# A hybrid encoder layer in three-product fp32: one of the weight sums of the seven-product pairs moved from VectorE to an accumulating GpSimd transfer, and the split of the sums it belongs to moved to the end

## The chip, the cores and the metric

One core of one Trainium2 chip runs the whole layer in one launch. The metric is the device time of that launch in microseconds (us), lower is better. Beside the plain times there is one profiled execution, from which all rows below are taken.

The core's engines are named as in the profile: PE is TensorE's matmuls (PEld its weight loads), DVE is VectorE, ACT is ScalarE, POOL is GpSimd, SP is the engine whose queue issues the loads. Each engine works through its own instructions in a fixed order and waits on semaphores for the others.

## The reference

The input is `x` of 256 tokens by 2048 float32. The layer is: a SwiGLU feed-forward block, a mixer (a gated linear recurrence beside a windowed attention, between one input and one output projection), and a second SwiGLU block, each between two RMS norms:

```python
def swiglu(x, w_gate_up, w_down):
    gate, up = jnp.split(x @ w_gate_up, 2, axis=-1)
    return (jax.nn.silu(gate) * up) @ w_down
...
ff = swiglu(rms_norm(x, pre_norm_ffn1[layer]), w_ffn1_gate_up[layer], w_ffn1_down[layer])
x = x + 0.5 * rms_norm(ff, post_norm_ffn1[layer])
h = rms_norm(x, pre_norm_mix[layer])
... # recurrence and attention on h @ w_mix_in[layer]
mixed = jnp.concatenate([y_h.astype(x.dtype), y_a.astype(x.dtype)], axis=-1) @ w_mix_out[layer]
x = x + rms_norm(mixed, post_norm_mix[layer])
# and the second SwiGLU block, again with 0.5
```

The weights are what is large: `w_ffn*_gate_up` is 2048 x 11264 and `w_ffn*_down` 5632 x 2048, twice, `w_mix_in` 2048 x 6656, `w_mix_out` 2048 x 2048, all float32.

## The kernel before

**Three products for one.** The matmuls run in fp32r (a float32 rounded to fewer bits). Each operand is therefore split into a high part `h`, rounded by ACT, and a low part `l`, the rest, which DVE takes (`split_act`, lines 176 and 177). A product of two operands is then three matmuls, h by h, h by l and l by h (`Blocks.three`, line 441). All weights have to be loaded from HBM, rounded by ACT and subtracted by DVE before PE can use them.

**Units.** The two feed-forward projections and the output projection work in units of 256 rows of the weight (two tiles of 128 rows) by 1024 columns (two blocks of 512). One unit is one `raw` tile of 128 partitions by 2048 columns that holds the four blocks b11, b12, b21, b22 side by side. There are three buffers for `raw`, five for `h` and five for `l` tiles of 1024 columns (a half of a `raw` tile each). `load` is issued on SP's queue when a `raw` buffer comes free.

A plain unit (`Blocks.plain`) multiplies eight times: two tokens' halves m, two column blocks n, two row tiles k. With three matmuls each that is 24 matmuls, and two split halves.

**Seven-product pairs.** Some units (the mixed ones: units 2, 4 and 6 of the eight of a gate/up group, ten of 22 in each run of the down projection, two of eight in each run of the output projection) are done with Winograd's form of Strassen's scheme, in `Blocks.seven`: seven products instead of eight, 21 matmuls, for sums of the left and of the right operand. The left sums are kept. The sums of the weights have to be made for each pair, in place in `raw`:

- b11 is split first, alone (`one_block`). 
- Line 473 is one DVE instruction on 1024 columns: b11 becomes b11 + b12, and b12 becomes b12 + b22.
- `lower` is the split of the second half of `raw`, still b21 and b22.
- Line 477 makes b22 = b11 + b22, with the new b11.
- `upper` is the split of the first half, b11 + b12 and b12 + b22.
- Line 479 makes b21 = b22 + b21, with the new b22.
- `last` is the split of the second half again, now with the sums.

So the four `h`/`l` tiles of a pair are those of b11, `lower`, `upper` and `last`, in this order, and PE multiplies in this order too: p0 with b11, two products with `lower`, two with `upper`, two with `last`.

**The order of the work.** Outside of a few hand-written stretches a scheduler decides at build time in which order each engine's instructions stand; on the chip the order is fixed. `aside` is a call that puts the load and the first split of the next unit between the steps of a pair; it is used where the next unit is a plain one and belongs to the same call of `work`, which is so in the down and output projections and not in the gate/up groups, whose units are called one by one.

**A gate/up group** is one pass of the eight units over 1024 columns (512 of gate, 512 of up). There are eleven groups in each feed-forward block. At the group's end `fold` adds the seven products to the banks of the plain ones: ACT copies one bank (line 522) and DVE does eight additions (lines 516 to 539), of which line 520 is the last that reads the product banks. Then the gate goes through Silu and times up (lines 959 and 960), PE transposes the result, and it is split for the down projection, with its sums (lines 395 to 399).

**GpSimd** does little: a few small loads and constants at the start and mid-layer, and the powers for the norms.

Of the kernel before, what the change touches and what calls it, by code (L numbers as in the profile page):

```python
# [17 lines left out]
ALU = mybir.AluOpType  # L18
AX = mybir.AxisListType

P = 128
# [16 lines left out]
def hymba_layer_kernel(  # L38
# [25 lines left out]
    nc = tc.nc  # L64
# [11 lines left out]
    def nm(s):  # L76
        uid[0] += 1
        return f"{s}_{uid[0]}"

    def pa():  # L80
        return psum.tile([P, 512], F32, tag="pa", name=nm("pa"))

    def pb():
        return psum.tile([P, 512], F32, tag="pb", name=nm("pb"))
# [56 lines left out]
    def load(src, between=None):  # L141
        raw = rawp.tile([P, 2048], F32, tag="raw", name=nm("raw"))
        if len(src.shape) == 4:

            dst = raw.rearrange("p (a n b) -> p a n b", a=src.shape[1], n=src.shape[2])
            parts = [(dst[:, a], src[:, a]) for a in range(src.shape[1])]
        else:
            parts = [(raw.rearrange("p (a b) -> p a b", a=src.shape[1]), src)]
        for i, (to, of) in enumerate(parts):
            if i and between:  # L150
                between()
            nc.sync.dma_start(to, of)
        return raw
# [14 lines left out]
    def split_half(raw, i, hp=hip, lp=lop):  # L168
        part = raw[:, i * 1024 : (i + 1) * 1024]
        h = hp.tile([P, 1024], F32R, tag="h", name=nm("h"))  # L170
        l = lp.tile([P, 1024], F32R, tag="l", name=nm("l"))
        split_act(h, l, part)
        return h, l

    def split_act(hi, lo, src):
        nc.scalar.copy(hi, src)  # L176
        nc.vector.tensor_tensor(lo, src, hi.bitcast(F32), ALU.subtract)  # L177
# [37 lines left out]
    last = {}  # L215
# [175 lines left out]
    S2, S3, S4, S1 = range(4)  # L391
# [10 lines left out]
    class Blocks:  # L402
# [60 lines left out]
        def seven(self, u, aside=None):  # L463

            raw = load(self.source(u))
            if aside:
                aside()
            b11, b12, b21, b22 = (raw[:, i * 512 : (i + 1) * 512] for i in range(4))
            four = raw.rearrange("p (i c) -> p i c", i=4)
            h, l = self.one_block()  # L470
            split_act(h, l, b11)

            nc.vector.tensor_tensor(  # L473
                four[:, 0:2], four[:, 0::3], four[:, 1:2].to_broadcast([P, 2, 512]), ALU.add
            )
            lower = split_half(raw, 1)
            nc.vector.tensor_tensor(b22, b11, b22, ALU.add)
            upper = split_half(raw, 0)
            nc.vector.tensor_tensor(b21, b22, b21, ALU.add)  # L479
            if aside:  # L480
                aside()
            last = split_half(raw, 1)
            if not self.p:
                self.p = [pa(), pa(), pb(), pb()]
            a, w = self.tiles[u], self.left_sums(u)

            def lhs(k, m):
                return [a[:, k, i, m * P : (m + 1) * P] for i in range(2)]

            def summed(j):  # L490
                return [w[:, j, i, :] for i in range(2)]

            def rhs(two, n):
                return [x[:, n * 512 : (n + 1) * 512] for x in two]

            for at, left, right in (
                (("p", 0), lhs(0, 0), (h, l)),
                (("c", 0, 0), lhs(1, 0), rhs(lower, 0)),
                (("c", 0, 1), summed(S4), rhs(lower, 1)),
                (("p", 1), summed(S1), rhs(upper, 0)),  # L500
                (("p", 3), summed(S3), rhs(upper, 1)),
                (("p", 2), summed(S2), rhs(last, 1)),
                (("c", 1, 0), lhs(1, 1), rhs(last, 0)),
            ):
                self.three(at, *left, *right)

# [79 lines left out]
    class Pairs(Blocks):  # L586
# [24 lines left out]
        def source(self, u):  # L611
            src = self.w[u * 2 * P : (u + 1) * 2 * P, self.now * 1024 : (self.now + 1) * 1024]
            return src.rearrange("(k p) c -> p k c", p=P)

        def left_sums(self, u):
            if u in self.kept:
                return self.kept[u]
            keep = self.now == 0 and u in self.keep
            if keep and u in self.near:
                w = self.room.tile([P, 4, 2, P], F32R, tag="sp", name=nm("sp"), bufs=3)  # L620
            else:
                tag = f"sp{u}" if keep else "sp"
                w = far["pool"].tile([P, 4, 2, P], F32R, tag=tag, name=nm("sp"), bufs=1 if keep else 2)
            split_act(w[:, :, 0, :], w[:, :, 1, :], self.sums[u])
            if keep:
                self.kept[u] = w
            return w
# [222 lines left out]
    class Gated(Blocks):  # L850
# [10 lines left out]

        def source(self, u):
            return self.w[:, 2 * u : 2 * u + 2, :, self.g * 512 : (self.g + 1) * 512]

        def left_sums(self, u):
            return self.sums[u]
# [171 lines left out]
    with tc.manual_schedule():  # L1038
# [9 lines left out]
        raw = rawp.tile([P, 2048], F32, tag="raw", name=nm("raw"))  # L1048
# [121 lines left out]
    with ExitStack() as s2:  # L1170
# [399 lines left out]
        rows = Pairs(w_mix_out[0], orders, yt, ysums, yroom, post_norm_mix)  # L1570
# [84 lines left out]
```

## Time and profile before

| what | value |
|---|---|
| median of 3 runs | 1836.45 us (1835.72 to 1837.55) |
| the profiled execution: span from first to last instruction | 1835.7 us |
| the profiled execution's own time beside that span | not listed apart from it; the span lies 0.75 us below the median |
| mean granted TensorE clock in it | 0.999 |
| PE busy | 1821.5 us (99%) |
| DVE busy | 1620.7 us (88%) |
| ACT busy | 1099.7 us (60%) |
| POOL busy | 23.3 us (1%) |
| DMA engines, loads of SP's queue | 56.0% of 16 engines' span, 364.17 MB |
| instructions of line 473, one for each seven-product pair | 102 |

The busy time of an engine is the time in which at least one of its instructions runs. Matmuls overlap in PE's pipeline, so that "99% busy" only says that there was hardly a moment without one. In the rows of groups the columns are line, engine, operation, tiles out<-in with their shapes, and count; then busy us and mean ns of one; then idle time before them and what ended it. In a timeline a row is a start in us, a duration in us, engine, line, operation, tiles, and xN where N instructions follow each other without a gap; in brackets stands the engine's idle time before it and its releaser.

### The profile page before, as it was taken

Reading aid. Unit: us, or ns where it says so; the run is one execution under the profiler, and the core shown is the slowest. Engines: PE = TensorE matmul, PEld = TensorE weight load, DVE = VectorE, ACT = ScalarE, POOL = GpSimd, SP = SyncE. Lnnn points to the kernel's source line nnn. Section 1 sums busy time; section 2 is a strip of 40 time slices with the busy share of each in tenths; the row PEclk is TensorE's granted clock in tenths of the full one; section 3 lists DMA queues with packets and bytes.
Section 4 is the critical chain, followed back from the end, with each engine's and each line's share of the span. In section 5 each row is a group of like instructions: output and inputs, shape, how many; then the busy total and the mean of one; then the engine's idle time right before and its main releaser. Section 6 shows DMA issues by size and latency. Waiting matters only on the chain.

```text
span 1835.7 us, 22980 instructions
## 1 busy us (share of the span) xinstructions
PE 1821.5 (99%) x8492; PEld 1516.5 (83%) x8492; DVE 1620.7 (88%) x2047; ACT 1099.7 (60%) x1454; POOL 23.3 (1%) x39
## 2 busy tenths in 40 slices
PE   9999999999999999999999999999999999999998
PEld 7888888888888888888888888888888888888786
DVE  7989999999999998477787798989999999999897
ACT  7555555555666567476587556455556555566563
POOL 1000000000000001000000000000000000000000
PEclk9999999999999999999999999999999999999999
DMA  7555555556555576555454456555555555545564
GB/s 255 206 178 213 207 200 191 184 188 215 205 208 216 195 260 212 199 182 174 163 170 150 167 210 224 190 195 190 213 193 192 213 212 195 205 187 206 201 229 177
DMA packets 174737, 365.77 MB, mean 199 GB/s; under 512 B 9256, under 2 KB 44160, under 8 KB 173856
## 3 DMA queue, kind: packets, MB, share of 16 engines
q1 hardware_dynamic: 174272, 364.17, 56.0%
q8 instruction: 66, 1.08, 0.2%
q14 instruction: 47, 0.39, 0.1%
q0 software_dynamic: 352, 0.14, 0.0%
HBM read 360.06 MB, written 4.21 MB: 198 GB/s over the span
## 4 chain that ended last, share of the span: by engine, by line
PE 94%; ACT 2%; DVE 2%; DMA 1%; issue 0%; POOL 0%; DVEq 0%; SPq 0%; ACTq 0%; POOLq 0%
PE pa L441 40%; PE pb L441 36%; PE pa L309 5%; PE pa L314 3%; PE pa L364 2%; PE pa L362 2%; PE pa L363 2%; DMA raw<-in_w_ffn_down_dram 1%; DVE l L177 1%; ACT h L176 1%; PE pb L971 1%; PE pa L971 1%; PE pb L1376 0%; PE pb L1350 0%; PE pb L1454 0%
## 5 line engine op out<-in xcount | busy, mean ns | idle before, releaser
L176 ACT CAST h<-raw 128x1024 fp32r<-128x1024 f32 (+1 forms) x825 | 821.5, 1021 | 538.2 <-PE pb L441 146.9
L177 DVE TENSOR_TENSOR l<-raw,h 128x1024 fp32r<-128x1024 f32 (+1 forms) x825 | 950.1, 1180 | 135.7 <-ACT h L176 106.0
L441 PE MATMUL pa<-h,xt 128*128 128x512 f32 x1176 | 409.5, 390 | 0.1
L441 PE MATMUL pb<-h,xt 128*128 128x512 f32 x1060 | 376.9, 392 | 0.0
L441 PEld LDWEIGHTS pa<-h,xt 128*128 128x128 f32 x1176 | 220.8, 188 | 46.1 <-DVE xt L232 0.6
L441 PEld LDWEIGHTS pb<-h,xt 128*128 128x128 f32 x1060 | 199.0, 188 | 41.6 <-DVE pb L537 0.6
L441 PE MATMUL pa<-l,xt 128*128 128x512 f32 x588 | 229.2, 390 | 0.0
L441 PE MATMUL pb<-l,xt 128*128 128x512 f32 x530 | 206.4, 389 | 0.0
L441 PE MATMUL pb<-h,ht 128*128 128x512 f32 x464 | 163.5, 390 | 0.0
L441 PE MATMUL pa<-h,ht 128*128 128x512 f32 x464 | 162.7, 389 | 0.0
L441 PEld LDWEIGHTS pa<-l,xt 128*128 128x128 f32 x588 | 110.4, 188 | 23.4 <-DVE l L177 0.8
L473 DVE TENSOR_TENSOR raw<-raw 128x1024 f32<-128x1024 f32 x102 | 124.3, 1219 | 1.1
L309 PE MATMUL pa<-xt,h 128*128 128x512 f32 x512 | 124.4, 393 | 0.2 <-ACT h L176 0.2
L441 PEld LDWEIGHTS pb<-l,xt 128*128 128x128 f32 x530 | 99.6, 188 | 19.6
L309 PEld LDWEIGHTS pa<-xt,h 128*128 128x128 f32 x512 | 93.8, 188 | 18.6 <-ACT h L176 0.6
L441 PEld LDWEIGHTS pa<-h,ht 128*128 128x128 f32 x464 | 87.1, 188 | 18.1
L441 PEld LDWEIGHTS pb<-h,ht 128*128 128x128 f32 x464 | 87.1, 188 | 18.0
L441 PE MATMUL pb<-l,ht 128*128 128x512 f32 x232 | 90.3, 389 | 0.0
L441 PE MATMUL pa<-l,ht 128*128 128x512 f32 x232 | 90.3, 389 | 0.0
L441 PE MATMUL pa<-h,xs 128*128 128x512 f32 x232 | 80.8, 389 | 0.0
L441 PE MATMUL pb<-h,xs 128*128 128x512 f32 x232 | 80.8, 389 | 0.0
L479 DVE TENSOR_TENSOR raw<-raw 128x512 f32<-128x512 f32 x102 | 70.1, 688 | 1.8
(281 smaller groups left out, 2360.6 us busy)
## 6 DMA issues: line engine op xcount, KB each, us to landing
raw<-in_w_ffn_gate_up_dram SPq DMA_DIRECT2D x350, 512.0 KB, 4.7
raw<-in_w_ffn_down_dram SPq DMA_DIRECT2D x88, 1024.0 KB, 5.0
raw<-in_w_mix_in_dram SPq DMA_DIRECT2D x52, 1024.0 KB, 4.9
raw<-in_w_mix_out_dram SPq DMA_DIRECT2D x16, 1024.0 KB, 4.9
pg<-in_post_norm_ffn_dram SPq DMA_DIRECT2D x4, 512.0 KB, 7.4
X<-in_x_dram SPq DMA_DIRECT2D x2, 1024.0 KB, 8.4
bias<-row SPq DMA_DIRECT2D x16, 128.0 KB, 5.0
kept<-X SPq DMA_DIRECT2D x2, 1024.0 KB, 4.1
```

What stands on the lines that cost most here:

```text
L176: nc.scalar.copy(hi, src)
L177: nc.vector.tensor_tensor(lo, src, hi.bitcast(F32), ALU.subtract)
L309: nc.tensor.matmul(slot[f], weights(hs, kk, f), xcol(xt, k), start=(k == 0), stop=(k == KT - 1))
L314: nc.tensor.matmul(slot[f][:, 0:T], weights(ls, kk, f), xcol(xt, kh * 8 + kk, 0), start=False, stop=False,)
L362: nc.tensor.matmul(dst, xh, h[:, o : o + n], start=(k == 0), stop=False)
L363: nc.tensor.matmul(dst, xh, l[:, o : o + n], start=False, stop=False)
L364: nc.tensor.matmul(dst, xl, h[:, o : o + n], start=False, stop=(k == KT - 1))
L441: nc.tensor.matmul(self.bank(at), lhs, rhs, start=(n == 1), stop=n in (ends, self.of[at]), skip_group_check=n > ends,)
L473: nc.vector.tensor_tensor(four[:, 0:2], four[:, 0::3], four[:, 1:2].to_broadcast([P, 2, 512]), ALU.add)
L479: nc.vector.tensor_tensor(b21, b22, b21, ALU.add)
L971: nc.tensor.transpose(bank[:, o : o + P], zs[m][:, k * P : (k + 1) * P], ident)
```

## The change

The one DVE instruction of line 473 becomes one of half its width, b11 = b11 + b12, and an accumulating transfer issued by GpSimd: it reads the block b22 (128 x 512 float32, 256 KB) from HBM a second time and adds it to b12 in SBUF. It depends on the addition before it, which reads b12, and the split `upper` depends on it. The split `upper` is put behind the split `last`, and the second `aside` behind `last` too. The order of the products follows: the two with `last` come ahead of the two with `upper`. A new method `block` gives the address of one 128 x 512 block for each of the two kinds of weight.

```diff
             h, l = self.one_block()
             split_act(h, l, b11)
 
-            nc.vector.tensor_tensor(
-                four[:, 0:2], four[:, 0::3], four[:, 1:2].to_broadcast([P, 2, 512]), ALU.add
-            )
+            nc.vector.tensor_tensor(b11, b11, b12, ALU.add)
+            nc.gpsimd.dma_start(b12, self.block(u, 1, 1), accum_op=ALU.add)
             lower = split_half(raw, 1)
             nc.vector.tensor_tensor(b22, b11, b22, ALU.add)
-            upper = split_half(raw, 0)
             nc.vector.tensor_tensor(b21, b22, b21, ALU.add)
+            last = split_half(raw, 1)
             if aside:
                 aside()
-            last = split_half(raw, 1)
+            upper = split_half(raw, 0)
...
                 (("c", 0, 1), summed(S4), rhs(lower, 1)),
+                (("c", 1, 0), lhs(1, 1), rhs(last, 0)),
+                (("p", 2), summed(S2), rhs(last, 1)),
                 (("p", 1), summed(S1), rhs(upper, 0)),
                 (("p", 3), summed(S3), rhs(upper, 1)),
-                (("p", 2), summed(S2), rhs(last, 1)),
-                (("c", 1, 0), lhs(1, 1), rhs(last, 0)),
...
+        def block(self, u, k, n):
+            rows, cs = (2 * u + k) * P, self.now * 1024 + n * 512
+            return self.w[rows : rows + P, cs : cs + 512]
...
+        def block(self, u, k, n):
+            return self.w[:, 2 * u + k, n, self.g * 512 : (self.g + 1) * 512]
```

In the changed kernel the three additions stand at lines 472, 475 and 476 and the transfer at line 473; the lines of `fold` move up by two, those behind `block` move down by three and five. In the order that the scheduler makes of it, the instructions of PE, DVE and ACT are as many as before, and `upper` stands in each pair where `last` stood, on DVE, on ACT and on PE.

More of the change, by code (lines that the diff above doesn't have):

```diff
@@ L468, in seven @@
             b11, b12, b21, b22 = (raw[:, i * 512 : (i + 1) * 512] for i in range(4))
-            four = raw.rearrange("p (i c) -> p i c", i=4)
             h, l = self.one_block()
             split_act(h, l, b11)
-            nc.vector.tensor_tensor(
-                four[:, 0:2], four[:, 0::3], four[:, 1:2].to_broadcast([P, 2, 512]), ALU.add
-            )
+            nc.vector.tensor_tensor(b11, b11, b12, ALU.add)
+            nc.gpsimd.dma_start(b12, self.block(u, 1, 1), accum_op=ALU.add)
             lower = split_half(raw, 1)
             nc.vector.tensor_tensor(b22, b11, b22, ALU.add)
-            upper = split_half(raw, 0)
             nc.vector.tensor_tensor(b21, b22, b21, ALU.add)
+            last = split_half(raw, 1)
             if aside:
                 aside()
-            last = split_half(raw, 1)
+            upper = split_half(raw, 0)
             if not self.p:
```

## The prediction

> **What bounds the kernel now.** I read the page's busy times and its chain of waits first, then the busy times of whole stages, then the timelines of DVE, ACT and PE over one gate/up group.
>
> ```profile
> PE 1821.5 (99%) x8492; PEld 1516.5 (83%) x8492; DVE 1620.7 (88%) x2047; ACT 1099.7 (60%) x1454; POOL 23.3 (1%) x39
> PE 94%; ACT 2%; DVE 2%; DMA 1%; issue 0%; POOL 0%; DVEq 0%; SPq 0%; ACTq 0%; POOLq 0%
> ```
>
> ```profile
> 50.00:480.00 430.00, 430.00 (x1937) 356.49 (x1936) 397.54 (x462) 243.90 (x280) 0.00 (x0) 1.00 0.56 200
> 480.00:720.00 240.00, 239.34 (x1067) 197.41 (x1067) 229.48 (x276) 147.06 (x192) 1.58 (x3) 1.00 0.59 216
> 1110.00:1590.00 480.00, 479.85 (x2174) 397.75 (x2173) 438.72 (x542) 274.93 (x351) 3.06 (x4) 1.00 0.55 197
> 1590.00:1822.00 232.00, 230.72 (x1021) 190.40 (x1020) 219.03 (x249) 137.62 (x164) 0.00 (x0) 1.00 0.56 209
> 358.79:401.16 42.37, 42.37 (x192) 35.18 (x192) 39.42 (x48) 24.42 (x29) 0.00 (x0) 1.00 0.56 199
> ```
>
> The columns of the windows are length, then busy time and count of PE, PEld, DVE, ACT and POOL, then clock, DMA share and GB/s. The first two rows are the gate/up groups and the down runs of the first feed-forward block, the next two those of the second, the last is one gate/up group. PE is without a gap in the gate/up groups, and lacks 0.66 + 0.15 + 1.28 us in the other three stretches. 94% of the chain is PE. A busy PE could still be a slow one, so I look at its starts.
>
> ```profile
> 357.02 0.39 PE L441 MATMUL pa<-h,xt 128*128 128x512 f32 x1
> 357.25 0.39 PE L441 MATMUL pb<-h,xt 128*128 128x512 f32 x1
> 357.48 0.39 PE L441 MATMUL pa<-h,xt 128*128 128x512 f32 x1
> ```
>
> They follow at 0.23 us. A group has 3 pairs of 21 matmuls and 5 plain units of 24, 183 in all; at 0.2265 us that is 41.4 us of the group's 42.37, and the transposes fill the rest. So the group is as long as its matmuls, and DVE, though 93% busy (39.42 of 42.37), runs just ahead of PE. What relieves DVE is worth nothing here beyond the 2.1 us that PE lacks, 0.1% of the time; what delays DVE by more than its lead is paid in full.
>
> **The change, part by part.** The DVE work:
>
> ```profile
> L473 DVE TENSOR_TENSOR raw<-raw 128x1024 f32<-128x1024 f32 x102 | 124.3, 1219 | 1.1
> L479 DVE TENSOR_TENSOR raw<-raw 128x512 f32<-128x512 f32 x102 | 70.1, 688 | 1.8
> ```
>
> Each of 102 pairs changes a 1219 ns addition for one of half the width, 688 ns by the other additions of that form: 0.53 us less, 54 us of DVE in all. PE, ACT and SP's queue keep their instructions. As PE is the bound this gives at most the 2.1 us above.
>
> In its place each pair gets one transfer of 256 KB, 102 x 0.26 = 27 MB on top of the loads. At a DMA share of 0.56 that lifts the share by some 4 to 8 points (the larger if reading the destination counts too); SP's loads have room for it, and I cost it at nothing. POOL, 1% busy, only issues; its powers for the norms come in stretches where no transfer is pending ahead of them.
>
> What counts is a wait: `upper` may start only when the transfer has landed, L after the end of the addition. ACT's copy waits for it, and behind this copy stand, on ACT and then on DVE, all later splits, the group's fold and Silu. `upper` stands in the place that `last` had on ACT, DVE and PE, so I compare the landing with the start of the copy of `last` before.
>
> ```profile
> 344.67 4.63 DVE L177 TENSOR_TENSOR l<-raw,h 128x1024 fp32r<-128x1024 f32 x4 [1.20 <-ACT h L176]
> 356.33 0.68 DVE L520 TENSOR_TENSOR s<-pa,z 128x512 f32<-128x512 f32 x1
> 358.79 1.21 DVE L473 TENSOR_TENSOR raw<-raw 128x1024 f32<-128x1024 f32 x1
> 367.72 5.23 DVE L177 TENSOR_TENSOR l<-raw,h 128x1024 fp32r<-128x1024 f32 x5 [1.17 <-ACT h L176]
> 372.87 1.22 DVE L473 TENSOR_TENSOR raw<-raw 128x1024 f32<-128x1024 f32 x1
> 380.87 1.23 DVE L473 TENSOR_TENSOR raw<-raw 128x1024 f32<-128x1024 f32 x1
> ```
>
> ```profile
> 366.63 4.42 ACT L176 CAST h<-raw 128x1024 fp32r<-128x1024 f32 x5 [1.93 <-DVE raw L479]
> 375.65 3.76 ACT L176 CAST h<-raw 128x1024 fp32r<-128x1024 f32 x4 [0.40 <-DVE raw L479]
> 385.95 3.00 ACT L176 CAST h<-raw 128x1024 fp32r<-128x1024 f32 x3 [2.70 <-DVE raw L479]
> ```
>
> The three pairs of the group start at 358.79, 372.87 and 380.87. The copies of `last`, which waited for line 479, started 7.84, 2.78 and 5.08 us later. The landing comes 0.69 + L after the same start. So:
>
> - First pair: free up to L = 7.15. Its fixed order has ten other DVE instructions between. The shorter addition and the end of ACT's wait of 1.93 us also let DVE come to the second pair earlier, by 0.53 to 0.53 + 1.17 (its idle time in the row at 367.72). I take 0.53, since the splits behind wait for tiles that PE still reads.
> - Second pair: late by 0.69 + L - 2.78 - 0.53 = L - 2.62. In the changed order only the two additions and one split stand between, 0.7 + 0.7 + 1.2 us.
> - Third pair: it starts with DVE as late as the second left it, since DVE's splits between are nearly solid. Its own lateness is 0.69 + L - 5.08 = L - 4.39.
>
> The sum is 2L - 7.0 at the third pair's last split. From there to line 520 (the same stretch a group earlier, from 344.67 to 356.33) DVE is solid as well, so line 520 is as late. It reads a product bank; PE's first matmul into the next group's second bank waits for it, at 357.48, where line 520 ended at 356.33 + 0.68 = 357.01. The lead is 0.47 us. PE then loses s = 2L - 7.5 us in each such group, if that is positive, after which the lateness is gone with the first pair's idle time. This order of three pairs, the second with the short distance, stands in the fourth to the eleventh group of each block: 16 groups.
>
> Now L, which no row of before shows. The nearest rows:
>
> ```profile
> raw<-in_w_ffn_gate_up_dram SPq DMA_DIRECT2D x350, 512.0 KB, 4.7
> X<-in_x_dram SPq DMA_DIRECT2D x4, 256.0 KB, 5.0
> out_dram<-X SPq DMA_DIRECT2D x8, 256.0 KB, 2.7
> bias_rows<-in_onehot_dram POOLq DMA_DIRECT2D x1, 64.0 KB, 4.3
> rows<-rn_lower_bounds_fwd_dram POOLq DMA_DIRECT2D x2, 4.0 KB, 5.4
> row<-bias_rows POOLq DMA_DIRECT2D x1, 16.0 KB, 1.8
> ```
>
> ```profile
> GB/s 0 0 0 0 0 0 0 0 0 0 0 0 0 131 213 139 311 369 385 393 369 410 393 369 369 385 377 393 393 401 393 336 295 328 418 320 229 180 90 25
> ```
>
> The last number of each is us from issue to landing. POOL's loads took 1.8 where little else moved, else 4.3 to 5.4 even for few KB; the very shape of this transfer (256 KB, 128 x 512) took 5.0 from SP in a full queue and 2.7 in an idle one, to HBM. The GB/s row is 367 to 377 us in 40 slices: where the second pair's transfer starts, at 373.6, the loads run at 377 to 400 GB/s. So the queue is full and I take L = 5.0, the row of the same size and shape. From below L is at least 1.8; from above nothing in the trace bounds an accumulation, which also reads what it adds to. I carry 3.5 to 6.5.
>
> With L = 5.0: s = 2.5 us, times 16 = 40 us. L = 4 gives 8, L = 6 gives 72, L = 6.5 gives 88.
>
> The down runs and the output projection, 44 pairs:
>
> ```profile
> 497.13 1.22 DVE L473 TENSOR_TENSOR raw<-raw 128x1024 f32<-128x1024 f32 x1
> 502.51 1.06 ACT L176 CAST h<-raw 128x1024 fp32r<-128x1024 f32 x1 [0.30 <-DVE raw L479]
> ```
>
> The copy of `last` started 5.38 us after the pair's start, in a stage where DVE's idle time is 10.5 us of 240 for 20 pairs, 0.53 each. Late by 0.69 + L - 5.38 = L - 4.69, less 0.53 saved and 0.53 idle: nothing at L = 5.0, 0.25 us a pair (11 us) at 6, 0.75 (33 us) at 6.5. The first groups of each block have wide distances or one more split between; I give them 1 us at L = 5.0, with PE's regained time against it.
>
> The sum is 1835.7 + 40 + 1 = 1876.7 for the profiled execution. Its span lies 0.75 us under the median of the runs, well within the rest, so I say 1877.
>
> One rule bears on L. The Trainium skill, "DMA: Bandwidth & Descriptors", section "Anatomy of one DMA — SWDGE (gpsimd) path", puts a GpSimd transfer at 2.0 us plus its bytes over 436 GB/s; an estimate from it is 2.6 us for 256 KB, by which s is negative and the time unchanged. POOL's loads of few KB at 4.3 to 5.4 us speak against it where the queue is full, the 1.8 us row for it.
>
> **The rivals.**
>
> *The transfer lands within its cover.* If L is under 3.75, 2L - 7.5 is not positive, nothing waits in any group, and the kernel isn't slower: 1836, or 1834 with PE's 2.1 us back. For it: the 2.7 us of 256 KB and POOL's 1.8 in quiet stretches. Against it: the second and third pair issue in the middle of a load. The formula of the skill quoted above would have this case. Chance 0.15.
>
> *The accumulation is slow.* If the transfer takes over 6.5 us, because its issue, its second read or its turn among the loads is longer than the plain rows, the down runs pay as well. L = 7: 16 x 6.5 + 44 x 1.25 = 159 us, 1995; at 8: 16 x 8.5 + 44 x 2.25 plus 16 x 0.85 from the first pairs, 249 us, 2085. For it: the 7.8 us that 512 KB of `x` took at the start, the worst in the same queue:
>
> ```profile
> X<-in_x_dram SPq DMA_DIRECT2D x2, 512.0 KB, 7.8
> ```
>
> Against it: half the bytes. Beside it stands a rule: the Trainium skill, "Collectives: The Full Stack", section "The bandwidth ceiling: the fold count and why AG ≠ RS ≠ AR", says that an add in the DMA engines needs two source reads and so runs at half the rate; no run here shows it yet. Chance 0.16.
>
> *DVE's relief counts.* If PE's even starts hid waits for DVE, 54 us less of DVE would show as time. PE's gapless windows speak against it; 1830 at best. Chance 0.03.
>
> **How the numbers follow.** The forecast, L from 3.75 to 6.5, has 0.66; the rivals 0.15, 0.16 and 0.03. Its own range is 1837 to 1836 + 88 + 33 = 1957. The range reaches down over the first rival to 1834 and, since L beyond 6.3 is thinly likely in the forecast, up to 1945 (16 x 5.1 + 44 x 0.55 = 106 over 1836, rounded up). That leaves out the slow rival and little else. About 0.2% is what a measurement of this kernel can tell from no change. Faster 0.03; the same 0.15; slower 0.82.
>
> **What would show it.** Right: in the profile of the changed kernel the transfer's row shows about 5 us to landing; ACT's copies wait for it by 2 to 3 us in the second pairs and not in the first; DVE's busy time falls by 54 us; PE has one gap of some 2.5 us a group, ended by DVE's line that was 520 (now 518); a group takes about 45 us and not 42.4; the down runs keep their length. Wrong: a landing under 3.75 or over 6.5 us, PE's gaps at the splits of `upper` instead of at the fold, or down runs that are longer although L is near 5.

## The result, and the profile after

The changed kernel takes 2027.5 us (median of four runs, 2025.2 to 2031.1) against 1836.2 us for the kernel before in the same comparison: a ratio of 1.104, with a 95% interval from 1.103 to 1.106. The forecast was slower, 1877 us with a range up to 1945; it is slower, but by 191 us and not by 40. The profiled execution of the changed kernel has a span of 2023.2 us.

First the page of the changed kernel: its busy times, GpSimd's DMA queue, the chain that ended last, and the rows of transfers (KB each, us from issue to landing).

```profile
PE 1892.1 (94%) x8492; PEld 1525.5 (75%) x8492; DVE 1579.4 (78%) x2047; ACT 1086.0 (54%) x1454; POOL 111.8 (6%) x141
q0 software_dynamic: 15040, 26.88, 8.1%
PE 41%; DMA 23%; DVE 20%; issue 8%; ACT 6%; SPq 0%; ACTq 0%; POOLq 0%; DVEq 0%; POOL 0%
raw<-in_w_ffn_gate_up_dram SPq DMA_DIRECT2D x350, 512.0 KB, 4.8
raw<-in_w_ffn_down_dram SPq DMA_DIRECT2D x88, 1024.0 KB, 5.4
raw<-in_w_ffn_gate_up_dram POOLq DMA_DIRECT2D x58, 256.0 KB, 4.8
raw<-in_w_ffn_down_dram POOLq DMA_DIRECT2D x40, 256.0 KB, 5.5
```

The chain was 94% PE and is 41% PE now; DMA has 23% of it, from 1%. The gate/up loads of SP's queue land in 4.8 us, as good as before (4.7). Those of the down weights take 5.4 us (5.0 before), and 5.5 us in the run below that has the new order and no transfer, so the added traffic isn't seen to disturb them. The new transfers take 4.8 and 5.5 us (medians) from GpSimd's issue to the landing, close to the 5.0 that the forecast took. But the issue isn't the end of the addition. The chain of waits inside one gate/up group shows the second pair's wait piece by piece (start, length, what):

```profile
409.86 0.61 DVE raw L472
410.47 0.03 POOLq L473
410.50 0.59 issue
411.10 4.36 DMA raw<-in_w_ffn_gate_up_dram
415.49 0.04 ACTq L176
415.52 0.04 issue
415.56 1.06 ACT h L176
```

From the end of the addition (410.47) to the start of ACT's copy of `upper` (415.56) it is 5.1 us: 0.6 until GpSimd's issue, 4.4 of transfer, the rest until ACT starts. The third pair of the same group is longer. ACT's and DVE's timelines:

```profile
415.56 4.42 ACT L176 CAST h<-raw 128x1024 fp32r<-128x1024 f32 x5 [2.49 <-DMA raw<-in_w_ffn_gate_up_dram]
428.37 2.94 ACT L176 CAST h<-raw 128x1024 fp32r<-128x1024 f32 x3 [3.15 <-DMA raw<-in_w_ffn_gate_up_dram]
```

```profile
420.78 0.69 DVE L472 TENSOR_TENSOR raw<-raw 128x512 f32<-128x512 f32 x1
421.39 1.22 DVE L177 TENSOR_TENSOR l<-raw,h 128x1024 fp32r<-128x1024 f32 x1
429.45 3.50 DVE L177 TENSOR_TENSOR l<-raw,h 128x1024 fp32r<-128x1024 f32 x3 [2.97 <-ACT h L176]
441.11 0.68 DVE L518 TENSOR_TENSOR s<-pa,z 128x512 f32<-128x512 f32 x1
```

The addition ends at 421.47, the copy starts at 428.37: 6.9 us. Below I call this distance, from the end of the addition to the start of ACT's copy of `upper`, L; it is what the forecast's landing was compared with. Over fifteen of the forecast's sixteen groups (all but the first block's fourth), L is 5.7 us on average in second pairs (5.05 to 6.96 from the 10th to the 90th percentile) and 7.0 in third pairs; over the forty pairs of the down runs it is 7.0 (5.4 to 9.6).

What PE waits for, by its weight loads (us in total, times, longest), and the busy times of three stretches: one gate/up group, the last group and the first down run (length, then PE, PEld, DVE, ACT and POOL, then granted clock, DMA share, GB/s).

```profile
PEld pa L441 <- ACT h L176: 75.8, 53, 5.3
PEld pa L441 <- DVE l L177: 74.6, 91, 1.1
PEld pa L441 <- DVE s L518: 19.8, 16, 2.1
```

```profile
396.48:443.57 47.09, 43.78 (x192) 34.86 (x191) 38.33 (x47) 24.07 (x29) 2.65 (x3) 1.00 0.63 196
491.10:539.99 48.89, 46.74 (x201) 37.77 (x200) 39.32 (x47) 26.27 (x33) 2.65 (x3) 0.97 0.61 197
539.99:774.56 234.57, 208.26 (x856) 162.33 (x854) 176.56 (x210) 113.54 (x135) 16.71 (x19) 0.97 0.61 198
```

This group takes 47.1 us where one took 42.37. The wait at the fold (line 518) is there, 16 times, but it is the smallest of the three: most waits stand at the splits themselves, because with a late `upper` PE catches up with ACT and DVE at once. The first down run, from its first to its twentieth addition, takes 234.6 us; the same stretch took 188.4 before (487.78 to 676.16).

Since every one of these kernels starts its 8492 matmuls in the same stages, the start of a given matmul can be compared between two traces. The table gives, for each kernel of this study, how many us it lost against the kernel before in each stage of its profiled execution (the borders are the 2200th, 3150th, 5600th and 7350th matmul; the last of them lies at 1566.7 us of before, in the last gate/up group of the second block, so that the last column of the changed kernel holds 5.8 us of that group):

| kernel | median us | gate/up 1 | down 1 | middle | gate/up 2 | down 2 |
|---|---|---|---|---|---|---|
| changed | 2027.5 | 52.1 | 45.6 | 0.6 | 40.4 | 48.6 |
| new order, wide addition | 1860.4 | 1.7 | 9.0 | 0.1 | 1.7 | 10.9 |
| the same, c product last | 1858.4 | 0.1 | 9.7 | 0.0 | 0.6 | 10.4 |
| plain load, SP's queue | 1881.8 | 6.6 | 15.4 | 0.1 | 6.3 | 15.0 |
| plain load, GpSimd's queue | 1964.9 | 29.2 | 35.3 | 0.0 | 26.8 | 34.3 |
| half the transfer | 1957.7 | 32.0 | 28.2 | 0.2 | 25.2 | 33.1 |
| addition behind `lower`'s split | 2034.7 | 46.4 | 48.9 | 1.1 | 40.8 | 56.6 |
| transfer ahead of the additions | 1902.2 | 2.4 | 33.0 | 0.1 | -0.1 | 28.4 |
| the same, gate/up only | 1837.9 | 2.2 | -0.3 | 0.1 | -0.1 | -0.9 |
| changed form in first pairs only | 1836.2 | -0.5 | -0.8 | 0.1 | 0.0 | -1.7 |
| changed form in down runs and output projection only | 1930.8 | -0.3 | 45.2 | 0.6 | 0.0 | 46.3 |

The mixer and the output projection (middle) lose 1.1 us at most.

### The profile page after: what moved, and what is told of

Read it like the earlier page. It is cut to its first block, busy times and chain, and to the rows that moved or that the text cites. A ratio compares the mean times of both kernels' runs of the same rounds, so it can differ in the third digit from the quotient of the medians.

```text
span 2023.2 us, 23501 instructions
## 1 busy us (share of the span) xinstructions
PE 1892.1 (94%) x8492; PEld 1525.5 (75%) x8492; DVE 1579.4 (78%) x2047; ACT 1086.0 (54%) x1454; POOL 111.8 (6%) x141
## 3 DMA queue, kind: packets, MB, share of 16 engines
q1 hardware_dynamic: 174272, 364.17, 52.1%
q0 software_dynamic: 15040, 26.88, 8.1%
## 4 chain that ended last, share of the span: by engine, by line
PE 41%; DMA 23%; DVE 20%; issue 8%; ACT 6%; SPq 0%; ACTq 0%; POOLq 0%; DVEq 0%; POOL 0%
PE pa L441 14%; DMA raw<-in_w_ffn_gate_up_dram 14%; DVE l L177 12%; PE pb L441 12%; DMA raw<-in_w_ffn_down_dram 9%; ACT h L176 5%; PE pa L309 5%; PE pa L314 2%; DVE raw L472 2%; PE pa L364 2%; PE pa L362 2%; PE pa L363 2%; DVE la L177 1%; DVE s L515 0%; DVE xt L935 0%
## 5 line engine op out<-in xcount | busy, mean ns | idle before, releaser
L176 ACT CAST h<-raw 128x1024 fp32r<-128x1024 f32 (+1 forms) x825 | 812.3, 1019 | 691.7 <-DVE raw L476 262.6
L441 PE MATMUL pa<-h,xt 128*128 128x512 f32 x1176 | 416.7, 396 | 13.5 <-DVE s L518 13.4
L441 PEld LDWEIGHTS pa<-h,xt 128*128 128x128 f32 x1176 | 225.0, 191 | 67.7 <-DVE s L518 19.8
L441 PE MATMUL pa<-l,xt 128*128 128x512 f32 x588 | 233.7, 397 | 0.5 <-DVE l L177 0.5
L441 PE MATMUL pa<-h,xs 128*128 128x512 f32 x232 | 93.9, 405 | 25.6 <-ACT h L176 25.6
L473 POOL DMA_DIRECT2D raw<-in_w_ffn_gate_up_dram x58 | 50.9, 877 | 896.2 <-DMA raw<-in_w_ffn_gate_up_dram 581.4
L441 PE MATMUL pa<-h,sp 128*128 128x512 f32 x176 | 73.3, 416 | 28.0 <-ACT h L176 27.9
L441 PE MATMUL pb<-h,xs 128*128 128x512 f32 x232 | 94.0, 405 | 0.0
```

The source lines that it names most:

```text
L441: nc.tensor.matmul(self.bank(at), lhs, rhs, start=(n == 1), stop=n in (ends, self.of[at]), skip_group_check=n > ends,)
L473: nc.gpsimd.dma_start(b12, self.block(u, 1, 1), accum_op=ALU.add)
```

## Experiments

**The order alone.** The new order of splits and products, with the old wide addition in place of the narrow one and the transfer:

```diff
+            four = raw.rearrange("p (i c) -> p i c", i=4)
...
-            nc.vector.tensor_tensor(b11, b11, b12, ALU.add)
-            nc.gpsimd.dma_start(b12, self.block(u, 1, 1), accum_op=ALU.add)
+            nc.vector.tensor_tensor(
+                four[:, 0:2], four[:, 0::3], four[:, 1:2].to_broadcast([P, 2, 512]), ALU.add
+            )
```

> Keeps the new order of splits and products but forms both sums with the one wide VectorE addition of the kernel before, so no transfer is issued. Theory 1 (the time from the narrow addition's end to the landing of the accumulated quarter is the whole cost): 1836 us, within 4 us of the kernel before, VectorE's busy time back by about 54 us. Rival 2 (the new order itself costs, since the half with the sums is split last): the time stays well above 1850 us, up to 2027 us if the order is all of it.

Measured: 1860.4 us, ratio 1.013 (1.011 to 1.015). Neither expectation in full: the order costs 24 us, 20 of them in the down runs. ACT's timeline of this kernel shows two pairs of a down run:

```profile
637.14 3.90 ACT L176 CAST h<-raw 128x1024 fp32r<-128x1024 f32 x4 [4.10 <-DVE raw L478]
647.75 3.90 ACT L176 CAST h<-raw 128x1024 fp32r<-128x1024 f32 x4 [4.12 <-DVE raw L478]
```

In both ACT stands for 4.1 us until the third addition (line 478) is done. The old second half, `upper`, needed only the wide addition; `last`, in its place now, needs the two narrow ones as well. Over the forty pairs its copy starts 3.24 us after the wide addition's start, where `upper`'s started after 1.33, and what is left between its finished split and PE's use falls from some 4 to 0.3 us (medians).

**The same with the c product at the end.** Only the order of the splits is kept:

```diff
-                (("c", 1, 0), lhs(1, 1), rhs(last, 0)),
                 (("p", 2), summed(S2), rhs(last, 1)),
                 (("p", 1), summed(S1), rhs(upper, 0)),
                 (("p", 3), summed(S3), rhs(upper, 1)),
+                (("c", 1, 0), lhs(1, 1), rhs(last, 0)),
```

> As the run with the new order and the wide addition (1860 us), but the product of the first quarter of last stands at the end of the pair again, as in the kernel before; only the order of the two splits, and of the products that depend on it, is left of the change. If the 24 us of the order come from the products that the fold waits for standing last: 1840 us or less. If they come from the second half's split being behind both narrow additions, 0.69 us later in every pair, mostly in the down runs: 1855 to 1865 us.

Measured: 1858.4 us, ratio 1.012 (1.011 to 1.014). So it is the order of the splits; where the products stand has about 2 of the 24 us.

**The accumulation.** A plain load in its place, on the same queue:

```diff
-            nc.gpsimd.dma_start(b12, self.block(u, 1, 1), accum_op=ALU.add)
+            nc.gpsimd.dma_start(b12, self.block(u, 1, 1))
```

> The transfer stays on GpSimd's queue, same bytes and same place, but it doesn't accumulate: b12 is overwritten by b22, so the sum b12 + b22 is left out. Theory 1 with a landing that is late because of issue, descriptors and neighbours: about 2027 us, within 10 us. Rival 3 (the accumulation itself is slow: its packets took 176 ns at the median against 84 ns for those of the plain loads, which is about 1.2 us of the 2.25 us from first to last packet): the landing comes about 1 us earlier, which by 2 us a group over 16 groups and 1 us a pair over the 44 other pairs is about 75 us less, 1950 us.

Measured: 1964.9 us, 62.6 less than the changed kernel and nearer to the rival's 1950 than to 2027. From its page:

```profile
q0 software_dynamic: 8512, 26.88, 4.0%
raw<-in_w_ffn_gate_up_dram POOLq DMA_DIRECT2D x58, 256.0 KB, 4.4
raw<-in_w_ffn_down_dram POOLq DMA_DIRECT2D x40, 256.0 KB, 4.9
```

The same 26.88 MB take 4.0% of 16 engines' 1961.4 us, 1255 us, where the accumulating ones took 8.1% of 2023.2, 2622 us: an accumulated byte costs the DMA engines 2.1 times a plain one. It isn't the size of the packets: an accumulating packet of 2 KB takes 178 ns, a plain one of 2 KB in SP's queue 84 ns, and plain ones of 4 KB take 159 ns in either queue (medians). L falls to 5.0 in second and 5.9 in third pairs, and the groups to 45.7 us. This is the rival "the accumulation is slow", in part: it has about a third of the loss. The rule of the Trainium skill beside that rival in the prediction, that an add in the DMA engines reads two sources and runs at half the rate, agrees with this factor; that a second read is the reason, no run here shows.

**The queue.** The same plain load from SP's queue:

```diff
-            nc.gpsimd.dma_start(b12, self.block(u, 1, 1), accum_op=ALU.add)
+            nc.sync.dma_start(b12, self.block(u, 1, 1))
```

> The same plain load (the sum b12 + b22 is left out), issued by SyncE's queue at the same place in the program instead of GpSimd's. Rival 4 (GpSimd's way of issuing is the cost: 0.64 us from the addition's end to the issue and 1.6 to 4 us to the first packet): the landing comes 1.5 to 3 us earlier and the time falls to between 1840 and 1930 us. Against it: the wait now stands in the queue of the big loads, ahead of the next pair's, and if that holds them up the time stays over 1950 us. If the landing time is set by the memory and the neighbours alone, 2027 us.

Measured: 1881.8 us, within what the rival gave, 83 less than from GpSimd's queue and 21 more than the new order without any transfer.

```profile
raw<-in_w_ffn_gate_up_dram SPq DMA_DIRECT2D x62, 256.0 KB, 3.8
raw<-in_w_ffn_down_dram SPq DMA_DIRECT2D x40, 256.0 KB, 4.3
```

The issue now starts 0.03 us after the addition and not 0.65, and the landing comes 0.6 us sooner after the issue. L is 3.7 and 4.6 in second and third pairs, for which the prediction's formula gives 0.8 us a group, and the groups are at 43.2 us. Whether the 21 us left over the order alone are all landing, or partly the wait that now stands in the queue of the big loads, the runs don't part.

**VectorE or the loads ahead of the transfer.** In the changed kernel the first packet comes 1.8 us after GpSimd's issue in second pairs and 2.95 us in third pairs (medians). In third pairs the 128x1024 subtraction of `lower` stands right behind the addition (421.39 in the timeline above), and VectorE works through the time; in second pairs it soon waits for ACT. Over all pairs the lag goes with the time that VectorE spends meanwhile on operations with two operands in SBUF (correlation 0.83; 0.92 us, and 0.87 us more for each us of it). This alone says little, since a longer lag also holds more of VectorE's work. To test it, the narrow addition was put behind `lower`'s subtraction:

```diff
...
-            nc.vector.tensor_tensor(b11, b11, b12, ALU.add)
-            nc.gpsimd.dma_start(b12, self.block(u, 1, 1), accum_op=ALU.add)
             lower = split_half(raw, 1)
+            with tc.issue_after(last_lo[0].ins):
+                nc.vector.tensor_tensor(b11, b11, b12, ALU.add)
+            nc.gpsimd.dma_start(b12, self.block(u, 1, 1), accum_op=ALU.add)
```

> As the changed kernel, but VectorE is made to do the narrow addition after the subtraction that ends lower's split, so that two narrow additions and no 128x1024 subtraction stand right behind it. The addition comes up to 1.2 us later, and so does the transfer's issue. Theory 5 (VectorE's work with two operands in SBUF holds up the making of GpSimd's descriptors: the lag from issue to first packet was 1.6 us in second pairs, 3.0 us in third pairs, which have that subtraction right behind the addition): the lag of third pairs falls to about 1.8 us, and the time is 2020 to 2035 us in spite of the later issue. Without such a hold-up the lag of third pairs stays near 3 us, and the later issue adds about 1.2 us a group and pair: over 2050 us.

(`last_lo` holds the last subtraction of a split; `issue_after` puts the addition behind it in VectorE's order.) Measured: 2034.7 us; the lag of third pairs is 1.7 us and L there 5.2 (medians; the 1.6 us that the expectation gives for second pairs is the lag of first pairs). The lag falls as expected, by 1.3 us, and the gain is eaten by the addition that comes 1.2 us later. But this doesn't show that VectorE holds the descriptors up, for the edit moved the transfer against SP's loads too. In third pairs of the changed kernel the last two loads were issued 1.95 and 1.36 us ahead of the transfer, in this run 2.96 and 2.38 us, much as in the second pairs of the changed kernel (3.02 and 2.44). Two transfers of the changed kernel part the two causes. In the 1.6 us from their issue VectorE does the same work (the end of a subtraction and the additions of lines 475 and 476), but in the second no load is running (DVE's busy time is the third figure, the DMA share the last but one):

```profile
422.10:423.70 1.60, 1.60 (x8) 1.33 (x8) 1.53 (x3) 0.00 (x0) 0.89 (x1) 1.00 1.04 398
668.04:669.64 1.60, 1.60 (x8) 1.31 (x7) 1.53 (x3) 0.62 (x1) 0.86 (x1) 1.00 0.02 3
```

The lag is 2.94 us in the first, a third pair, and 1.59 us in the second, a pair of a down run. Of the 102 transfers, 24 find SP's packets on less than half of the DMA engines' time from 0.8 to 1.6 us after their issue; none of these has a lag over 1.61 us, where the other 78 have 2.64 at the median. So no lag is long here without running loads; whether VectorE's work adds to it beside them, the runs don't part. The Trainium skill, "SBUF — State Buffer", section "SBUF: two separate sides", describes GpSimd as unable to write descriptors while VectorE holds the port pair that the two share, and names VectorE's two-port modes as the trigger. The transfer at 668.04 shows no such hold-up by VectorE's float32 operations of two operands.

**Half the transfer.** GpSimd's transfer adds the right 256 columns, VectorE the left:

```diff
-            nc.gpsimd.dma_start(b12, self.block(u, 1, 1), accum_op=ALU.add)
+            nc.gpsimd.dma_start(
+                b12[:, 256:512], self.block(u, 1, 1)[:, 256:512], accum_op=ALU.add
+            )
+            nc.vector.tensor_tensor(b12[:, 0:256], b12[:, 0:256], b22[:, 0:256], ALU.add)
```

> As the changed kernel, but the accumulating transfer covers only the right half of b12 (256 of 512 columns); VectorE adds the left half itself, a 128x256 addition of some 0.4 us. If the part of the landing from first to last packet (2.3 to 3.3 us) goes by bytes, the landing comes 1.1 to 1.6 us earlier, and by 2 us a group over 16 groups and about 1 us in each of 44 other pairs, less the added 0.4 us, the time falls to about 1940 to 1965 us. If it goes by the number of packets or descriptors (as many as before, of half the size), it stays at 2020 to 2040 us.

Measured: 1957.7 us, in the range for a landing that goes by bytes.

```profile
q0 software_dynamic: 15040, 13.51, 4.6%
raw<-in_w_ffn_gate_up_dram POOLq DMA_DIRECT2D x58, 128.0 KB, 4.1
```

As many packets, of half the size. But half the bytes take 0.7 us off the landing of 4.8 and 0.8 to 0.9 off L in second and third pairs, and not the 1.1 to 1.6 us that the expectation reckoned with: that the time came out is in part luck. A straight line through the two sizes gives the estimate that some 3.4 us of the landing don't go with the bytes: the larger part.

**The transfer without the wait.** The sums are formed in another order, so that b12 + b22 comes first and the transfer depends on the pair's load alone:

```diff
             raw = load(self.source(u))
+            b11, b12, b21, b22 = (raw[:, i * 512 : (i + 1) * 512] for i in range(4))
+            nc.gpsimd.dma_start(b12, self.block(u, 1, 1), accum_op=ALU.add)
...
             nc.vector.tensor_tensor(b11, b11, b12, ALU.add)
-            nc.gpsimd.dma_start(b12, self.block(u, 1, 1), accum_op=ALU.add)
             lower = split_half(raw, 1)
-            nc.vector.tensor_tensor(b22, b11, b22, ALU.add)
-            nc.vector.tensor_tensor(b21, b22, b21, ALU.add)
-            last = split_half(raw, 1)
+            nc.vector.tensor_tensor(b22, b11, b22, ALU.subtract)
+            upper = split_half(raw, 0)
+            nc.vector.tensor_tensor(b21, b11, b21, ALU.add)
             if aside:
                 aside()
-            upper = split_half(raw, 0)
+            last = split_half(raw, 1)
...
```

> The same accumulating transfer in every seven-product pair, but issued as soon as the pair's load has landed, ahead of all VectorE work on it: b12 becomes b12 + b22 first, and the other three sums are formed from it with three narrow operations (b11 + s2, s3 - b22, s3 + b21; same VectorE time as in the changed kernel), in the old order of halves and products. Theory 1 (what costs is the wait for a transfer that can start only after the pair's first addition, not its bytes, its packets or its queue): 1836 us, between 1832 and 1842 us, with VectorE about 54 us less busy. If the transfer's traffic or GpSimd's queue cost by themselves, or if the loads land too late to give the transfer its 5 us: over 1850 us, and ACT waits for the DMA of the pair's first quarter.

Measured: 1902.2 us, ratio 1.037 (1.036 to 1.039): outside the 1832 to 1842 that the theory gave. The table says where: 2.4 us and nothing in the gate/up stages, 33 and 28 in the down runs. There the condition named in the expectation holds, the load lands too late; the waits of DVE's first addition:

```profile
DVE raw L473 <- DMA raw<-in_w_ffn_down_dram: 76.7, 33, 6.0
```

The loads of the down weights are 1024 KB each and here take 6.4 us to land; a transfer that can start only after them comes after the time at which the addition was due.

**The same in the gate/up stages only.**

```diff
...
+            if not hasattr(self, "g"):
+                return self.seven_before(u, aside)
...
```

(`g` is a name that only the class of the gate/up groups has; `seven_before` is the old method.)

> The early transfer (issued when the pair's load has landed) in the pairs of the gate/up stages only, 58 of 102; the 44 pairs of the down runs and of the output projection as in the kernel before. With the early transfer everywhere the gate/up stages lost 2.4 us at their start and then nothing. Theory 1: 1836 us, within 4 us; VectorE's busy time about 30 us less than before. If the early form has a cost in the gate/up stages that the down runs' waits hid: over 1845 us. A gain over 2 us is not to be had, since TensorE lacks only 2 us in the kernel before.

Measured: 1837.9 us, ratio 1.0005 (0.9996 to 1.0014): no difference.

```profile
PE 1822.1 (99%) x8492; PEld 1518.3 (83%) x8492; DVE 1591.3 (87%) x2047; ACT 1104.8 (60%) x1454; POOL 73.1 (4%) x97
raw<-in_w_ffn_gate_up_dram POOLq DMA_DIRECT2D x58, 256.0 KB, 4.1
```

58 accumulating transfers of 256 KB from the same queue, and PE is at 99% again. They cost no more than some 2 us (the table's 2.2 at the start) when nothing on the path waits for them. And 29 us less of DVE bring nothing either: the rival "DVE's relief counts" is gone. No version run here is faster than the kernel before.

**The pairs with the long cover only.** The changed form where the prediction had put 7.15 us of cover, in the first pair of each group from the third on (18 pairs):

```diff
+            if not (hasattr(self, "g") and self.g > 1 and u == MIXED_IN[0]):
+                return self.seven_before(u, aside)
...
```

> The changed form only in the first pair of each gate/up group (14 or so of 102 pairs), all others as in the kernel before. These pairs have the longest cover: after the changed kernel's transfer its split's result still lies 1.8 us before TensorE's use. Theory 1: 1836 us, within 3 us. If the transfer costs anything beyond its landing (about 1.9 us per pair is what 191 us over 102 pairs would make): up to 1865 us.

Measured: 1836.2 us, ratio 1.000 (0.999 to 1.001). As expected.

**The other stages only.** The changed form in the down runs and the output projection, `if hasattr(self, "g")` in place of the condition above:

> The changed form in the 44 pairs of the down runs and of the output projection only, the gate/up pairs as in the kernel before. In the changed kernel the down runs lost 46 and 49 us, the output projection nothing. If the losses of the stages are independent: 1836 + 95 = 1931 us, within 6 us. If the down runs suffer from what the gate/up stages leave behind: under 1915 us.

Measured: 1930.8 us, ratio 1.052 (1.050 to 1.053). The losses of the stages are nearly independent: the down runs alone lose 94 us by the medians (91.5 in the two columns of the table), and 88 in the changed kernel once the last group's 5.8 us are taken from its last column. That the expected sum came out so well owes something to those 5.8 us in its 95.

## Why the prediction was wrong

*PE is the bound, and DVE's relief is worth nothing*: right. The additions' rows show 124.3 us before and 69.9 now, the 54 us forecast:

```profile
L472 DVE TENSOR_TENSOR raw<-raw 128x512 f32<-128x512 f32 x102 | 69.9, 686 | 1.1
```

*The traffic costs nothing*: right for the gate/up stages, by the run with the early transfers there; for the down runs no run shows it alone.

*First pairs are free up to L = 7.15*: not contradicted. Eighteen first pairs cost nothing at a landing of 4.0 us; an L near 7 didn't come up in them.

*s = 2L - 7.5 in each steady group*: the mechanism was right, and the size of L was the step that failed: 5.0 us in the forecast, 5.7 and 7.0 in second and third pairs. Written with an L for each pair, the formula is s = (L2 - 2.62) + (L3 - 4.39) - 0.47. The measured means of L (fifteen groups) and of the group's length (without each block's last) give:

| kernel | L2, L3 | 42.37 + s | measured group |
|---|---|---|---|
| changed | 5.74, 6.97 | 47.6 | 47.4 |
| half the transfer | 4.97, 6.03 | 45.9 | 45.8 |
| plain, GpSimd's queue | 4.99, 5.88 | 45.8 | 45.7 |
| plain, SP's queue | 3.66, 4.63 | 43.2 | 43.2 |

The forecast took one L of 5.0 for both, from an SP load's issue to its landing. It left out the 0.64 us between the addition and GpSimd's issue and the copy's start behind the landing; it left to a rival that an accumulating byte costs 2.1 times as much; and it gave both pairs the same L, where in third pairs the first packet comes 1.1 us later than in second pairs (2.95 and 1.84 us after the issue). The sixteen steady groups lost 82 us in place of 40. That PE pays at the fold was half right: most of the waiting moved to the splits of `upper`, which the prediction had listed as a sign against itself.

*The first groups of each block, 1 us*: wrong, 8.9 us before the fourth group of the first block and 7.0 in the second. There are five pairs ahead of it in each block, two in the first two groups and three in the third. PE took the split of `upper` the moment it was done in three of the first block's five (L from 5.2 to 7.0); these groups were not worked out.

*The down runs, L - 5.75 each, nothing at L = 5.0*: wrong, and not only in size. They lost 88 us, nearly half of the whole. Two steps failed. First, "`upper` stands in the place that `last` had" compared one half only: `last` took `upper`'s place as well and has to wait for two more additions there. The order alone costs 20 us in the down runs. Second, each pair was costed by itself, as if ACT and DVE kept their lead from pair to pair. They lose it. The chain of waits in a down run of the changed kernel, from one addition to the next (pieces of 0.04 us and less left out, but for two):

```profile
710.38 0.70 DVE raw L472
711.08 0.03 POOLq L473
711.11 0.59 issue
711.71 6.77 DMA raw<-in_w_ffn_down_dram
718.56 1.05 ACT h L176
719.63 0.04 DVE l L177
719.67 1.11 issue
720.77 0.68 DVE la L177
721.46 1.14 DVE l L177
722.60 0.61 DVE raw L472
723.24 0.59 issue
723.84 7.04 DMA raw<-in_w_ffn_down_dram
```

PE isn't in it. ACT takes its work in order, and the copies that the next pair's addition needs stand behind the copy of `upper`, which waits for the landing. So the wait closes on itself: from addition to addition it is 12.2 us here, 7.5 of it L and 4.7 the splits between and the addition. Over the forty pairs a pair takes 12.3 us on average, 5.3 more than its L of 7.0; with the plain load on GpSimd's queue 11.7, 5.4 more than its L of 6.3. Before, a pair took 9.9 us (188.4 us for 19 steps), with hardly a gap in PE. An estimate from these: the loop passes that at an L of about 4.6, and beyond it each pair pays every us of L. The other kernels don't fit it as well: with the load on SP's queue a pair takes 10.8 us and with half the transfer 11.3, both at an L of 6.3, and the new order without a transfer already takes 10.4. In SP's case the copy starts over 0.5 us behind the landing in 17 of the 40 pairs, so that something else holds it there. That the loop is the cause is read from the chain and from the periods of two kernels; no run cut it, and it stays open how much of the 88 us it has.

Put together, by the ladder of kernels in the table: 1836 us; 24 for the order; 21 for a plain load on SP's queue; 83 for GpSimd's queue in its place; 63 for the accumulation; 2027. (The order in which the steps are taken may shift their shares.) The rivals: "lands within its cover" fell, and with it the estimate of 2.6 us by the Trainium skill's formula for GpSimd's transfers ("DMA: Bandwidth & Descriptors", "Anatomy of one DMA — SWDGE (gpsimd) path"): the quickest of them in the changed kernel took 4.0 us from issue to landing (minimum, median and maximum of line 473):

```profile
DMA to landing us min/median/max: 4.0/5.4/9.9
```

"The accumulation is slow", with an L over 6.5 at a chance of 0.16, is the nearest of the four; its price of 1995 at L = 7 came near, in part by luck: it gave the down runs 55 us, for pairs costed one by one, and the first groups nothing. Two readings in the prediction are off without bearing on the sum: 7.8 us is not the longest landing in SP's queue (1024 KB of `x` took 8.4), and among GpSimd's small loads are two of 4.0 and 4.1 us.

## What to carry to other kernels

An instruction on a tight engine that is exchanged for a DMA on the path costs the whole distance from the producer's end to the consumer's start, here 5 to 7 us for 256 KB against a 0.53 us saving; measure that distance and not the issue-to-landing column, and start the transfer from data that are ready long before (the same 58 transfers, issued at the load's landing, cost some 2 us at most). Before pricing a wait against a single slack, follow the waiting engine's queue around to the next producer: if the loop closes, the period can become the wait plus the work between, and a pair's own slack no longer covers it. And where a half takes another's place, compare what each of the two has to wait for.

## What the runs showed of the hardware

Besides the doubled cost of accumulated bytes and the lag behind running loads, the granted TensorE clock was not expected to move. Three windows of the changed kernel, columns as above:

```profile
474.80:478.20 3.40, 1.25 (x5) 0.48 (x3) 1.23 (x2) 2.31 (x3) 0.00 (x0) 0.99 0.03 6
478.20:481.60 3.40, 3.35 (x8) 2.68 (x9) 3.40 (x4) 3.01 (x4) 0.00 (x0) 0.50 0.53 158
481.60:485.00 3.40, 3.40 (x17) 2.78 (x16) 3.40 (x5) 1.06 (x1) 0.00 (x0) 1.00 1.04 378
```

After 3.4 us in which PE started five matmuls, the next 3.4 us run at a clock of 0.50, with 8 matmuls in them and not 15. This happens in 14 places of the changed kernel before its end, 55 us in all, so up to 27 of its 191 us are slower matmuls and not waits, by an estimate from the clock of 0.50; with the plain load on GpSimd's queue it is 24 us in five places, with the one on SP's a single one. By the same estimate up to 15 of the 63 us between the accumulating and the plain load are this. In the Trainium skill, "TensorE: Matmul & The Clock Gate", section "What's actually happening", a fixed window of about 3.4 us decides. This agrees with the 14 slow stretches, which are 3.41 or 6.83 us long. But it took no whole window without work: in the 3.41 us ahead of each of them PE started one to six matmuls, and was idle for 1.6 to 3.4 us.
